# Four edits to a two-layer encoder kernel: sixteen early dot products, a dense expert stage for 224 tokens, a later reload, and a top-k over 112 sums

## The chip, the cores and the metric

The kernel runs on one core of one Trainium2 chip. The core has a matmul engine (TensorE, "PE" in the profile; "PEld" is its loading of weights), a vector engine (VectorE, "DVE"), an activation engine (ScalarE, "ACT"), a general engine (GpSimd, "POOL") and a sync engine (SyncE, "SP") that here does nothing but start DMA transfers. Each engine works through its own queue in order and waits on semaphores for the others. The metric is the device time in microseconds.

## The reference

Two layers; in each a token mixer (a recurrent block in layer 0, a convolution block in layer 1) and then an expert block, with a layer norm behind each. 16 learned tokens are put ahead of the 256 of the input, so layer 0 works on 272 tokens and layer 1's mixer drops the 16. The change touches the expert block alone:

```python
def peer_block(xc, w_query, sub_keys, expert_u, expert_v):
    q = (xc @ w_query).reshape(c, PEER_HEADS, 2, PEER_HALF)
    scores = jnp.einsum('chpk,pnk->chpn', q, sub_keys.astype(q.dtype))
    s1, i1 = lax.top_k(scores[:, :, 0], PEER_TOPK)
    s2, i2 = lax.top_k(scores[:, :, 1], PEER_TOPK)
    cand = (s1[..., :, None] + s2[..., None, :]).reshape(c, PEER_HEADS, PEER_TOPK * PEER_TOPK)
    s, flat = lax.top_k(cand, PEER_TOPK)
    idx1 = jnp.take_along_axis(i1, flat // PEER_TOPK, axis=-1)
    idx2 = jnp.take_along_axis(i2, flat % PEER_TOPK, axis=-1)
    expert = idx1 * PEER_N_KEYS + idx2
    g = jax.nn.softmax(s.astype(jnp.float32), axis=-1).astype(xc.dtype)
    act = jax.nn.gelu(jnp.einsum('chkd,cd->chk', expert_u[expert], xc))
    return jnp.einsum('chk,chkd->cd', g * act, expert_v[expert])
```

There are 8 heads, 128 keys a half, so 16,384 experts; each head of a token picks 16 of them. All is float32, 1024 features wide.

## The kernel before

**Dense and gathered tokens.** Most tokens do not gather their experts. For them the block multiplies by all experts: first by U (128 tiles of 128 experts, each 512 KB), then it weighs the result by a matrix that holds the gates of the chosen experts and zeros elsewhere, then it multiplies by V (128 tiles again). `DENSE_U` and `DENSE_V` give how many tokens of a layer go through U and V in this way. The rest go by groups of 16 tokens (`FEW`), 8 heads x 16 tokens on the 128 partitions, 16 steps for their 16 choices: a dot product (a gather of 128 rows of U by an indirect DMA from POOL, `few_rows`, L1013, and one DVE product with a sum, `few_mult`, L1020) and an addition to the output (a gather of 128 rows of V and one DVE multiply-add, `few_add`, L1049). A group's output is folded into the accumulators by 8 narrow matmuls when it is whole (`few_step`, L1093, called in the V loop). There are three kinds. An **early** group (tokens from 256 in layer 0, from 240 in layer 1) has its first dots in the U stage and the rest in V. A **late** group (from 240 in layer 0) has them all in V. A **drawn** group (from 224 and from 208 in layer 1) goes through the dense U, whose activations are dumped to a table in DRAM (`few_dump`, L710, by POOL); in V its 16 activations are drawn from there by 16 small indirect DMAs (`few_draw`, L1030).

**Stages of a layer's expert block**, in order of the program (`peer`, L545): queries; top-k; U1 (tiles 0 to 63 of U); U2 (tiles 64 to 127, while the gates are built and multiplied in, 8 tokens a chunk, `g_unit`, L676); V (tiles 0 to 123, L753); the last four tiles of V in halves.

**A weight tile** (`load_split`, L138) is loaded by SP, rounded on ACT (`hi`), and the remainder `lo = raw - hi` is taken by DVE or POOL. U takes 24 matmuls a tile (hi by x, hi by the remainder of x, lo by x), and the eight with `lo` stand last. V takes 8 wide ones (hi by the weighted activations and their remainder side by side, twice `DENSE_V` columns) and 8 narrow ones (lo). `raw` has four buffers, `hi` three, `lo` two. In U1 POOL takes the remainders up to tile 40 and DVE from tile 41 (`LO_FROM`), since DVE is at the top-k until then; in U2 and V DVE takes all.

**Top-k** (`topk_steps`, L874) runs on DVE: 16 of 128 keys for 16 halves of heads, then 16 of 256 sums for each head, then the indices by one-hot products. The tokens from 128 on are done first, those from 0 to 127 after them; the last seven steps of the second set go one to a tile from tile 41. `softmax` (L932) makes the gates z from tile 54 on. The gates of groups below token 256 are turned to the groups' layout by way of DRAM: a POOL DMA writes (`few_spread`, L992), and another that waits for its landing reads (`few_fetch`, L996).

**Order.** A scheduler orders each engine's queue by what it thinks is ready; `issue_after(x)` holds instructions of the same engine as x behind x, and does nothing on other engines. So a DMA that POOL starts is not held by an ACT instruction. Steps of the gathered groups in V come from a table that `few_plan` (L1058) makes: rows of (group, dot or sum, step), spread evenly over tiles 2 to 111, the draws between.

## Time and profile before

| what | us |
|---|---|
| median of three runs (1806.37 to 1811.37) | 1810.56 |
| the profiled execution | 1811.96 |
| its span, first to last instruction | 1810.2 |
| U1 of layer 0: first and last activation stored | 178.1 and 350.1 |
| V of layer 0: first wide matmul | 553.0 |
| U1 of layer 1: first and last activation stored | 1095.3 and 1267.6 |
| V of layer 1: first wide matmul | 1466.5 |
| DVE busy | 1503.9 |
| ACT busy | 908.9 |
| POOL busy | 483.8 |

Matmuls overlap one another in the profile, so the busy time of one says little; the count of matmuls in a stretch without waits says how fast they follow each other. "Waited for" names what ended an engine's idle time. Times at a row's start are microseconds from the start of the span.

### The profile page before, as it was taken

What the parts mean: (1) busy time and instruction counts of PE and PEld (TensorE: products, weight loads), DVE (VectorE), ACT (ScalarE), POOL (GpSimd) and SP (SyncE); (2) the same over time, 40 slices, a digit from 0 to 9 for tenths busy, and PEclk for the clock granted to TensorE, in tenths of its full rate; (3) what the DMA queues carried; (4) which work ended last, traced back from release to release, by engine and by line L of the source; (5) the groups of instructions that cost most, each with busy time, mean ns of one, the idle gap of its engine ahead of it and who ended that gap; (6) DMA issues with size and microseconds to landing.
All of it is one profiled execution on the core that took longest, in us unless ns stands there. A gap on an engine that the chain in (4) does not pass through costs nothing.

```text
span 1810.2 us, 34904 instructions
## 1 busy us (share of the span) xinstructions
PE 1760.8 (97%) x13484; PEld 1685.9 (93%) x13484; DVE 1503.9 (83%) x2727; ACT 908.9 (50%) x1492; POOL 483.8 (27%) x328
## 2 busy tenths in 40 slices
PE   8999999999999999999998999999999999999996
PEld 7899999999999999999887899999999999999996
DVE  7786998889997777787699769998889968878875
ACT  5554444554445444885432645445454445544452
POOL 1102993100002332221000017962100035634210
PEclk9999999999999999999999999999999999999998
DMA  5446667755557888887541356578555568989973
GB/s 198 163 152 161 195 195 248 253 164 165 169 171 280 307 306 289 293 305 251 192 133 65 105 175 182 182 240 279 186 173 184 172 247 324 329 310 316 321 259 120
DMA packets 112439, 396.41 MB, mean 219 GB/s; under 512 B 13584, under 2 KB 14992, under 8 KB 112144
## 3 DMA queue, kind: packets, MB, share of 16 engines
q1 hardware_dynamic: 91632, 324.74, 53.7%
q0 software_dynamic: 20640, 69.43, 10.8%
q8 instruction: 106, 1.74, 0.4%
q14 instruction: 61, 0.50, 0.1%
HBM read 387.14 MB, written 6.98 MB: 218 GB/s over the span
## 4 chain that ended last, share of the span: by engine, by line
PE 82%; DVE 9%; DMA 3%; POOL 2%; issue 2%; ACT 1%; POOLq 0%; DVEq 0%; SPq 0%; ACTq 0%
PE u L180 40%; PE acc L732 21%; PE acc L736 12%; PE u L216 3%; DVE cy L1224 2%; POOL lo L152 2%; DVE odd L1224 2%; PE g L682 1%; PE g L683 1%; DVE lo L152 1%; DMA raw<-peer_v 1%; DMA rows<-u_rows,ids 1%; PE sps L578 1%; PE var L856 0%; PE acc L770 0%
## 5 line engine op out<-in xcount | busy, mean ns | idle before, releaser
L145 ACT ACTIVATE hi<-raw 128x1024 fp32r<-128x1024 f32 x556 | 588.6, 1059 | 625.3 <-PE u L180 190.9
L152 DVE TENSOR_TENSOR lo<-raw,hi 128x1024 fp32r<-128x1024 f32 x474 | 579.9, 1226 | 173.6 <-PE acc L736 74.7
L180 PE MATMUL u<-xs,hi 128*128 128x240 f32 (+2 forms) x4544 | 569.1, 277 | 0.6 <-DVE xs L379 0.6
L180 PEld LDWEIGHTS u<-xs,hi 128*128 128x128 f32 x4544 | 537.5, 189 | 1.5 <-DVE xs L379 1.2
L732 PE MATMUL acc<-w,hi 128*128 128x480 f32 (+1 forms) x1984 | 448.0, 368 | 4.8 <-ACT hi L145 2.9
L732 PEld LDWEIGHTS acc<-w,hi 128*128 128x128 f32 x1984 | 355.1, 189 | 29.2 <-ACT hi L145 3.2
L180 PE MATMUL u<-xs,lo 128*128 128x240 f32 (+2 forms) x2272 | 308.2, 277 | 5.4 <-POOL lo L152 3.2
L180 PEld LDWEIGHTS u<-xs,lo 128*128 128x128 f32 x2272 | 280.5, 189 | 7.5 <-POOL lo L152 4.2
L736 PEld LDWEIGHTS acc<-w,lo 128*128 128x128 f32 x2048 | 269.4, 191 | 13.5 <-DVE lo L152 5.8
L736 PE MATMUL acc<-w,lo 128*128 128x240 f32 (+1 forms) x2048 | 272.1, 274 | 4.4 <-DVE lo L152 4.4
L152 POOL TENSOR_TENSOR lo<-raw,hi 128x1024 fp32r<-128x1024 f32 x82 | 209.8, 2580 | 100.6 <-ACT hi L145 73.0
L1015 POOL DMA_INDIRECT rows<-peer_v,ids x80 | 122.3, 1529 | 237.6 <-DVE few_out L1056 171.6
L1015 POOL DMA_INDIRECT rows<-u_rows,ids x48 | 59.9, 1249 | 379.2 <-DVE act_b L702 216.0
L216 PE MATMUL u<-x,raw 128*128 128x272 f32 x480 | 114.7, 399 | 5.3 <-DMA x<-h 5.3
L216 PEld LDWEIGHTS u<-x,raw 128*128 128x128 f32 x480 | 92.9, 194 | 24.8 <-DMA raw<-w_in 5.2
L1056 DVE SCALAR_TENSOR_TENSOR few_out<-rows,act,few_out 128x1024 f32<-128x1024 f32 x75 | 96.0, 1280 | 0.0
L689 ACT ACTIVATE act_b<-g 128x432 f32<-128x432 f32 (+41 forms) x56 | 21.9, 390 | 108.8 <-DVE act_b L652 97.4
L665 DVE TENSOR_TENSOR AB<-iota,iT 128x2048 f16<-128x2048 f16 x56 | 68.1, 1219 | 0.1
L1022 DVE SCALAR_TENSOR_TENSOR rows<-rows,wide 128x1024 f32<-128x1024 f32 x48 | 58.5, 1219 | 4.2 <-DMA rows<-u_rows,ids 4.2
L682 PE MATMUL g<-AB 128*128 128x128 f16 x448 | 56.6, 220 | 0.0
L683 PE MATMUL g<-Bl,AB 128*128 128x128 f16 x448 | 56.0, 219 | 0.0
L713 POOL COPY own<-act_b 128x512 f32<-128x512 f32 (+2 forms) x6 | 5.4, 935 | 182.1 <-ACT act_b L698 182.1
(284 smaller groups left out, 1778.6 us busy)
## 6 DMA issues: line engine op xcount, KB each, us to landing
raw<-peer_u SPq DMA_DIRECT2D x256, 512.0 KB, 4.2
raw<-peer_v SPq DMA_DIRECT2D x248, 512.0 KB, 5.1
raw<-w_query SPq DMA_DIRECT2D x28, 512.0 KB, 4.0
raw<-pw SPq DMA_DIRECT2D x22, 512.0 KB, 3.5
raw<-w_in SPq DMA_DIRECT2D x16, 512.0 KB, 4.1
raw<-w_out SPq DMA_DIRECT2D x8, 512.0 KB, 3.9
raw<-peer_v SPq DMA_DIRECT2D x16, 256.0 KB, 4.5
wide<-wide SPq DMA_DIRECT2D x5, 512.0 KB, 4.3
```

The lines of the kernel that those rows point to most:

```text
L145: self.act_hi = nc.scalar.activation(hi, raw, AF.Copy).ins
L152: i = e.tensor_tensor(lo[:, s], raw[:, s], hi[:, s].bitcast(F32), op=OP.subtract)
L180: self.mm = nc.tensor.matmul(ps[:, :n], l[:, k, :], xs(k, r)[:, :n], start=start, stop=stop)
L216: self.mm = self.nc.tensor.matmul(ps[:, :n], raw[:, k, :], x[:, k, :n], start=k == 0, stop=k == NB - 1)
L665: nc.vector.tensor_tensor(AB.rearrange("p x c (a b) -> p (x c) a b", b=2), keys, iT[:, c0 // HC].rearrange("p x c b -> p (x c) b")[:, :, N ...
L682: nc.tensor.matmul(ps[:, c, :], A, Bh, start=True, stop=False)
L683: nc.tensor.matmul(ps[:, c, :], A, Bl, start=False, stop=True)
L732: self.mm = nc.tensor.matmul(acc[b][:, :2 * n].rearrange("p (a t) -> p a t", a=2), hi, w[:, :, :n], start=j == 0, stop=j == NK - JG - 1, s ...
L736: self.mm = nc.tensor.matmul(main[b][:, :n], hi if p_ else lo, w[:, i, :n], start=False, stop=j == NK - 1 and not p_, skip_group_check=True)
L1015: self.nc.gpsimd.indirect_dma_start(out=t, out_offset=None, in_=table, in_offset=bass.IndirectOffsetOnAxis(ap=few["ids"][:, i, k:k + 1], a ...
L1056: nc.vector.scalar_tensor_tensor(few["out"], t, w, few["out"], op0=OP.mult, op1=OP.add)
L1224: nc.vector.scalar_tensor_tensor(z, h, w, z, op0=OP.mult, op1=OP.add)
```

## The change

In layer 0 V becomes dense for 224 tokens instead of 240, and the group from 224 is drawn, as in layer 1. The early groups do all 16 dots in U1, from tile 41 on, four steps in five tiles; their gelu stands at the end of U1. From tile 42 on every third remainder of U1 is POOL's. The draws of V begin at tile 6, not 2. The reload of the block's input `xr` for the residual is held behind the load of V tile 119. The second search of the top-k goes over the 112 sums in which one of the two ranks is below 4 (a sum with both ranks 4 or more has at least 24 others that are no smaller), and the indices are worked out from the shorter list by four more DVE instructions.

```diff
-DENSE_U, DENSE_V = (240, 240), (240, 208)
-EARLY, LATE, DRAWN = ((256,), (240,)), ((240,), ()), ((), (224, 208))
-DOTS_FROM, DOTS, AHEAD, LO_FROM = 48, 10, 2, 41
+NEAR = 4
+DENSE_U, DENSE_V = (240, 240), (224, 208)
+EARLY, LATE, DRAWN = ((256,), (240,)), ((240,), ()), ((224,), (224, 208))
+DOTS_FROM, AHEAD, LO_FROM = 41, 2, 41
...
-            self.nc.sync.dma_start(raw[:, i * w:(i + 1) * w], part)
+            self.last_load = self.nc.sync.dma_start(raw[:, i * w:(i + 1) * w], part).ins
...
-                    if j == LO_FROM:
+                    if j == DOTS_FROM - 3:
                         for few in early:
                             self.few_load(sp, few, "kept", 1)
...
-                    k, step = divmod(3 * (j - DOTS_FROM), 4)
-                    if early and 0 <= k < DOTS + AHEAD and step < 3:
+                    k, step = divmod(4 * (j - DOTS_FROM), 5)
+                    if early and 0 <= k < TOPK + AHEAD and step < 4:
                         with tc.issue_after(self.dve_lo.ins), tc.issue_after(self.lo_ins.ins):
-                            self.few_dot(sp, early[0], k, DOTS, AHEAD)
+                            self.few_dot(sp, early[0], k, TOPK, AHEAD)
...
+                    if j == JA - 1:
+                        for few in early:
+                            nc.scalar.activation(few["act"], few["act"], AF.Gelu_apprx_tanh)
...
-                self.linears([U[j] for j in range(JA)], xs, nu, lambda j: FULL if j >= LO_FROM else (("p", 1024),), u_store)
+                self.linears([U[j] for j in range(JA)], xs, nu, lambda j: FULL if j >= LO_FROM and j % 3 else (("p", 1024),), u_store)
...
-                        for i in range(2):
-                            nc.sync.dma_start(xr[:, 4 * i:4 * i + 4, :], self.saved[:, 4 * i:4 * i + 4, :])
+                        with tc.issue_after(self.last_load):
+                            for i in range(2):
+                                nc.sync.dma_start(xr[:, 4 * i:4 * i + 4, :], self.saved[:, 4 * i:4 * i + 4, :])
...
-        cand = sp.tile([P, H, K, K], F32, tag="cand", name="cand", bufs=1)
-        nc.vector.tensor_tensor(cand[:m], sv[:m, :, 0, :, None].to_broadcast([m, H, K, K]),
-                                sv[:m, :, 1, None, :].to_broadcast([m, H, K, K]), op=OP.add)
+        cand = sp.tile([P, H, NEAR * K + (K - NEAR) * NEAR], F32, tag="near", name="cand", bufs=1)
+        for part, rows, cols in ((cand[:m, :, :NEAR * K], slice(0, NEAR), slice(0, K)),
+                                 (cand[:m, :, NEAR * K:], slice(NEAR, K), slice(0, NEAR))):
+            shape = [m, H, rows.stop - rows.start, cols.stop]
+            nc.vector.tensor_tensor(part.rearrange("p h (a b) -> p h a b", b=cols.stop),
+                                    sv[:m, :, 0, rows, None].to_broadcast(shape),
+                                    sv[:m, :, 1, None, cols].to_broadcast(shape), op=OP.add)
...
+        nc.vector.tensor_scalar(far, fp, cut, cut, op0=OP.max, op1=OP.subtract)
         nc.vector.tensor_scalar(pu[:m, 0], fp, 4, None, op0=OP.logical_shift_right)
-        nc.vector.tensor_scalar(pu[:m, 1], fp, 15, None, op0=OP.bitwise_and)
+        nc.vector.tensor_scalar(far, far, 2, None, op0=OP.logical_shift_right)
+        nc.vector.tensor_scalar(pu[:m, 1], fp, float(NEAR * K), float(K - NEAR), op0=OP.is_lt, op1=OP.mult)
+        nc.vector.tensor_tensor(pu[:m, 0], pu[:m, 0], far, op=OP.max)
+        nc.vector.scalar_tensor_tensor(pu[:m, 1], pu[:m, 1], NEAR - 1, fp, op0=OP.bitwise_or, op1=OP.bitwise_and)
...
-                for k in range((DOTS if few in early else TOPK if few["drawn"] else 0) if i == 0 else 0, TOPK)]
+                for k in range(0 if i or few in late else TOPK, TOPK)]
...
+            if s == ahead and not late:
+                self.warm(AF.Abs_reciprocal_sqrt)
...
-                        self.few_gelu(few, few is (early + late)[-1])
+                        self.few_gelu(few, few is late[-1])
...
-            lo, hi = begin + 14 * g, at[rows.index((few, 1, 0)) + ahead] - 3
+            lo, hi = 6 + 12 * g, at[rows.index((few, 1, 0)) + ahead] - 3
```

How the instructions stand now is seen at three places. First POOL in U1 of layer 0, from tile 24 of U on before: `rows` are the gathers of the early group, `z` first the write of the turned gates to DRAM and then the read of them.

```order
L152 TENSOR_TENSOR lo<-raw,hi 128x1024 x16
L1015 DMA rows<-u_rows,ids_1619 128x1024 x8
L994 DMA z_240_1627<-z 16x8x16
L998 DMA z_1624<-z_240_1627 128x16
L1015 DMA rows<-u_rows,ids_1619 128x1024 x8
```

The same place after the change, from the remainder of tile 51 on (the remainders below are those of tiles 51, 54, 57 and 60):

```order
L153 TENSOR_TENSOR lo<-raw,hi 128x1024
L1032 DMA rows<-u_rows,ids_1619 128x1024 x2
L153 TENSOR_TENSOR lo<-raw,hi 128x1024
L1032 DMA rows<-u_rows,ids_1619 128x1024 x3
L1011 DMA z_240_1627<-z 16x8x16
L1011 DMA z_224_1634<-z 16x8x16
L1015 DMA z_1624<-z_240_1627 128x16
L1015 DMA z_1630<-z_224_1634 128x16
L153 TENSOR_TENSOR lo<-raw,hi 128x1024
L1032 DMA rows<-u_rows,ids_1619 128x1024 x2
L153 TENSOR_TENSOR lo<-raw,hi 128x1024
```

Before, no remainder stood behind the gates' DMAs on POOL; now that of tile 57 does, with two writes and two reads ahead of it (three and three in layer 1). Second, DVE in U1 of layer 0, before, from the remainder of tile 43 to that of tile 52:

```order
L152 TENSOR_TENSOR lo<-raw,hi 128x1024
L924 TENSOR_TENSOR oh<-oh,s_3436 128x2048
L152 TENSOR_TENSOR lo<-raw,hi 128x1024
L924 TENSOR_TENSOR oh<-oh,s_3436 128x2048
L152 TENSOR_TENSOR lo<-raw,hi 128x1024
L927 TENSOR_REDUCE idx<-oh 128x128
L152 TENSOR_TENSOR lo<-raw,hi 128x1024
L927 TENSOR_REDUCE idx<-oh 128x128
L152 TENSOR_TENSOR lo<-raw,hi 128x1024 x4
L1022 SCALAR_TENSOR_TENSOR rows,act_1620<-rows,wide 128x1024
L152 TENSOR_TENSOR lo<-raw,hi 128x1024
```

And after, from the remainder of tile 44 to that of tile 49 (`rows,act` is a dot product):

```order
L153 TENSOR_TENSOR lo<-raw,hi 128x1024
L939 TENSOR_TENSOR oh<-oh,s_3462 128x2048
L1039 SCALAR_TENSOR_TENSOR rows,act_1620<-rows,wide 128x1024
L939 TENSOR_TENSOR oh<-oh,s_3462 128x2048
L1039 SCALAR_TENSOR_TENSOR rows,act_1620<-rows,wide 128x1024
L153 TENSOR_TENSOR lo<-raw,hi 128x1024
L942 TENSOR_REDUCE idx<-oh 128x128
L1039 SCALAR_TENSOR_TENSOR rows,act_1620<-rows,wide 128x1024
L153 TENSOR_TENSOR lo<-raw,hi 128x1024
L942 TENSOR_REDUCE idx<-oh 128x128
L1039 SCALAR_TENSOR_TENSOR rows,act_1620<-rows,wide 128x1024
L153 TENSOR_TENSOR lo<-raw,hi 128x1024
```

The dots now stand between the last steps of the top-k, where one remainder stood after each step before. Third, SP in layer 1, before, from the load of the early group's tokens (`wide`) in U1:

```order
L1043 DMA wide<-wide_240_12651 128x1024
L135 DMA raw<-peer_u 128x1024 x121
L135 DMA raw<-peer_v 128x1024 x6
L1043 DMA wide<-wide_240_12651 128x1024
L135 DMA raw<-peer_v 128x1024 x56
L759 DMA xr<-saved_11873 128x1024 x2
L135 DMA raw<-peer_v 128x1024 x62
```

and after:

```order
L1060 DMA wide<-wide_240_12747 128x1024
L136 DMA raw<-peer_u 128x1024 x121
L136 DMA raw<-peer_v 128x1024 x120
L764 DMA xr<-saved_11961 128x1024 x2
L136 DMA raw<-peer_v 128x1024 x4
```

The second `wide` of layer 1 is gone, and `xr` has moved from behind V tile 61 to behind V tile 119, where layer 0 had it before and has it now.

More of the change, by code (lines that the diff above doesn't have):

```diff
@@ L894, in topk_steps @@
         for h in range(H):
-            s = cand[:m, h].rearrange("p a b -> p (a b)")
+            s = cand[:m, h]
             v, i = fv[:m, h, :], fi[:m, h, :]
-            r = sp.tile([P, K * K], F32, tag="r2", name="r2", bufs=1)
+            r = sp.tile([P, NEAR * K + (K - NEAR) * NEAR], F32, tag="r2", name="r2", bufs=1)
             nc.vector.max(v[:, 0:8], s)
@@ L907, in topk_steps @@
         fp = fi[:m].rearrange("p h k -> p (h k)")
+        far = sp.tile([P, H * K], U32, tag="far", name="far", bufs=1)[:m]
+        cut = float(NEAR * K - NEAR * NEAR)
+        nc.vector.tensor_scalar(far, fp, cut, cut, op0=OP.max, op1=OP.subtract)
         nc.vector.tensor_scalar(pu[:m, 0], fp, 4, None, op0=OP.logical_shift_right)
-        nc.vector.tensor_scalar(pu[:m, 1], fp, 15, None, op0=OP.bitwise_and)
+        nc.vector.tensor_scalar(far, far, 2, None, op0=OP.logical_shift_right)
+        nc.vector.tensor_scalar(pu[:m, 1], fp, float(NEAR * K), float(K - NEAR), op0=OP.is_lt, op1=OP.mult)
+        nc.vector.tensor_tensor(pu[:m, 0], pu[:m, 0], far, op=OP.max)
+        nc.vector.scalar_tensor_tensor(pu[:m, 1], pu[:m, 1], NEAR - 1, fp, op0=OP.bitwise_or, op1=OP.bitwise_and)
         pf = sp.tile([P, 2 * H * K, 2], F16, tag="pf", name="pf", bufs=1)
@@ L953, in few_new @@
                "z": kp.tile([P, 1, TOPK], F32, name=f"z{t0}")}
+        if few["drawn"]:
+            few["turn"] = kp.tile([P, TOPK], U32, name=f"turn{t0}")
         if t0 < 2 * P:
@@ L1086, in few_plan @@
         for g, few in enumerate(drawn):
-            few["turn"] = vp.tile([P, TOPK], U32, name=f"turn{few['t0']}")
-            lo, hi = begin + 14 * g, at[rows.index((few, 1, 0)) + ahead] - 3
+            lo, hi = 6 + 12 * g, at[rows.index((few, 1, 0)) + ahead] - 3
             self.steps += [(lo + k * (hi - lo) // TOPK, lambda few=few, k=k: self.few_draw(few, k)) for k in range(TOPK)]
```

## The prediction

> **What bounds the kernel now.** I read the page's busy times first.
>
> ```profile
> PE 1760.8 (97%) x13484; PEld 1685.9 (93%) x13484; DVE 1503.9 (83%) x2727; ACT 908.9 (50%) x1492; POOL 483.8 (27%) x328
> ```
>
> PE is the bound nearly everywhere: it is busy for 97% of the span. So only two things count: how much PE has to do, and how long it waits. Work taken from DVE, such as the shorter top-k, is worth only what PE waited for it. Next I cut V into stretches and counted matmuls. Columns: stretch, length, busy us (count) of PE, PEld, DVE, ACT and POOL, granted clock, DMA share, GB/s.
>
> ```profile
> 595.00:685.00 90.00, 90.00 (x548) 81.82 (x548) 70.32 (x62) 44.59 (x44) 30.26 (x17) 1.00 0.84 304
> 1527.00:1590.00 63.00, 63.00 (x421) 62.71 (x420) 53.42 (x62) 33.73 (x34) 38.76 (x28) 1.00 0.91 331
> 1474.00:1490.00 16.00, 13.94 (x89) 13.36 (x89) 11.05 (x15) 5.29 (x6) 9.44 (x8) 1.00 0.94 348
> 1508.00:1518.00 10.00, 8.61 (x55) 8.23 (x55) 6.56 (x10) 6.11 (x7) 5.17 (x5) 1.00 0.74 270
> 1621.00:1632.00 11.00, 7.88 (x35) 7.10 (x34) 6.83 (x6) 5.43 (x6) 2.10 (x2) 0.69 0.69 257
> 1760.00:1776.00 16.00, 16.00 (x110) 15.94 (x109) 9.56 (x9) 9.00 (x9) 0.00 (x0) 1.00 0.62 200
> ```
>
> The first two are undisturbed V, of layer 0 (480 wide columns) and of layer 1 (416). The next three are layer 1's disturbances. The last is layer 1 when the gathers are over.
>
> **V of layer 0, narrower.** 90.00/548 x 16 = 2.628 us a tile at 480 columns, and 63.00/421 x 16 = 2.394 at 416. The new 448 is half-way, 2.511, so 0.117 less for each of 124 tiles: **-14.5 us**.
>
> ```profile
> L732 PE MATMUL acc<-w,hi 128*128 128x480 f32 x992 | 236.8, 381 | 1.0 <-DVE w L264 1.0
> L732 PE MATMUL acc<-w,hi 128*128 128x416 f32 x992 | 211.1, 355 | 3.8 <-ACT hi L145 2.9 <-DVE w L264 0.9
> L736 PE MATMUL acc<-w,lo 128*128 128x240 f32 x1024 | 136.4, 275 | 0.8 <-DVE lo L152 0.8
> L736 PE MATMUL acc<-w,lo 128*128 128x208 f32 x1024 | 135.7, 274 | 3.7 <-DVE lo L152 3.7
> L770 PE MATMUL acc<-same,few_out 128*128 128x16 f32 x80 | 9.3, 258 | 0.0
> ```
>
> Half the difference of the two wide rows is 12.8 us, the nearer end. The narrow rows are alike at 240 and 208 columns, so nothing comes from them or from the last four tiles, which have only that form. Whether V keeps that pace: layer 0 will gather 64 times in some 110 tiles, (512 KB x (1 + 64/110))/2.511 us = 330 GB/s, as the undisturbed stretch of layer 1 moves (331) without a wait. I add nothing; at 348 GB/s the stretch from 1474 did wait, so up to +5.
> The additional group costs one more fold: 9.3/80 x 16 matmuls = **+1.9**.
>
> **U2 of layer 0** has 28 chunks of gates instead of 30. A chunk stands between two tiles (first matmul of a chunk, and of the tile behind it):
>
> ```profile
> 400.57 0.23 PE L682 MATMUL g<-AB 128*128 128x128 f16 x1
> ...
> 401.45 2.04 PE L180 MATMUL u<-xs,hi 128*128 128x240 f32 x16
> ```
>
> Its matmuls take 401.45 - 400.57 = 0.88; two fewer give **-1.8**.
>
> **V of layer 1: three waits.** By 0.1496 us a matmul, the stretches lost 16.00 - 89 x 0.1496 = 2.7, then 10.00 - 55 x 0.1496 = 1.8, then 11.00 - 35 x 0.1496 = 5.8. Who was waited for, from the waits of 1470:1490, of 1506:1518 and of 1618:1632, with SP's own issue from the timeline:
>
> ```profile
> ACT hi L145 <- DMA raw<-peer_v: 7.9, 2, 6.7
> 1473.34 0.33 SPq L1043 DMA_DIRECT2D wide<-wide  x1
> DVE w L264 <- ACT w L261: 3.4, 1, 3.4
> ACT hi L145 <- DMA raw<-peer_v: 8.7, 4, 7.6
> 1610.82 0.80 SPq L759 DMA_DIRECT2D xr<-saved  x2
> ```
>
> In the first, V tiles came late behind `wide` and the first draws; layer 1 loses that load and draws from tile 6. In the second, ACT was at the early group's gelu; it moves to the end of U1. In the third, the 1 MB of `xr` joined a stage that already moves 331 GB/s; it moves to where 200 GB/s are moved (last stretch). All three should go: **-10.2**. If the new places brought the waits back it would be 0; layer 0 has `xr` at that place now without one.
>
> **U1, both layers.** Here a wait is added. POOL's queue and PE, first layer 0, then layer 1:
>
> ```profile
> 329.38 0.60 POOL L994 DMA_DIRECT2D z<-z  x1 [1.52 <-DVE z L947]
> 333.14 0.58 POOL L998 DMA_DIRECT2D z<-z  x1 [3.17 <-DMA z<-z]
> 331.10 1.06 PE L180 MATMUL u<-xs,lo 128*128 128x240 f32 x8
> 1253.48 0.54 POOL L998 DMA_DIRECT2D z<-z  x1 [1.45 <-DMA z<-z]
> 1249.77 1.06 PE L180 MATMUL u<-xs,lo 128*128 128x240 f32 x8
> L152 POOL TENSOR_TENSOR lo<-raw,hi x82: 2359/2402/4406, 160.0 to 1199.7; 128x1024 fp32r<-128x1024 f32 x82
> ```
>
> The gates are written by POOL, and the read stands until the write has landed. Now the remainder of tile 57 is queued behind this pair, and behind that the gathers and the remainder of tile 60. PE cannot go on: the eight `lo` matmuls of tile 57 began at 331.10 and 1249.77. With two pairs in layer 0 the reads end a trigger later, 333.14 + 0.58 + 0.6 = 334.3; 0.3 to start and 2.4 for the remainder give 337.0, so PE stands 5.9. In layer 1 the third read ends at 1254.02 already; plus 2.7 is 1256.7, PE stands 6.9. Together **+12.8**. This holds if DVE has the gates as early as now; I do not think so.
>
> ```profile
> 285.00:350.00 65.00, 64.27 (x571) 63.78 (x570) 56.24 (x82) 33.01 (x56) 9.84 (x11) 1.00 0.80 271
> L1022 DVE SCALAR_TENSOR_TENSOR rows<-rows,wide 128x1024 f32<-128x1024 f32 x48 | 58.5, 1219 | 4.2 <-DMA rows<-u_rows,ids 4.2
> 292.11 1.22 DVE L924 TENSOR_TENSOR oh<-oh,s 128x2048 f16<-128x2048 f16 x1
> 297.49 2.28 DVE L927 TENSOR_REDUCE idx<-oh 128x128 f32<-128x2048 f16 x1
> 296.35 1.23 DVE L152 TENSOR_TENSOR lo<-raw,hi 128x1024 fp32r<-128x1024 f32 x1 [0.33 <-ACT act_a L608]
> 1160.36 16.21 POOL L152 TENSOR_TENSOR lo<-raw,hi 128x1024 fp32r<-128x1024 f32 x6
> L890 DVE TENSOR_TENSOR cand<-sv x5: 2377/3319/16228, 183.4 to 1158.1; 128x2048 f32<-128x2048 f32 x4, 128x256 f32<-128x256 f32 x1
> rows<-u_rows,ids POOLq DMA_INDIRECT x48, 7.2
> ```
>
> A sum that takes 2.38 at least took 16.23, the one at 1158.1, while POOL ran six remainders: such DVE work stands while POOL's runs. From the remainder of tile 44 to that of 47 DVE now has two products (2 x 1.22), three dots (3 x 1.22), two remainders (2 x 1.23) and a reduction (2.28), 10.8, and 2.4 more while POOL takes tile 45: 13.2 for three tiles of 24 x 65.00/571 = 2.7, less one tile that the second `lo` buffer gives: 2.4 late. Then the tenth dot before the gates waits for rows gathered behind POOL's tile 54, which land 7.2 after issue: some 1.8 more. So 4.2 a layer, **+8.4**; none at the low end, rival C at the high one.
> The granted clock was 0.69 over 11 us around layer 1's waits of 2.2 and less, worth 3.4 at full loss; the new waits are longer. I take 2.2 for each, **+4.4**, between 0 and 6.8: part falls into the wait itself.
> [...]
> Against it stand PE's old waits behind this place (for `lo` of DVE and for the second gates), which a longer wait ahead of them gives DVE time to remove: 1.6 + 0.6 in layer 0, 0.9 in layer 1, **-3.0**:
>
> ```profile
> PEld u L180 <- DVE lo L152: 1.6, 1, 1.6
> PEld tps L1105 <- DVE z L947: 1.2, 2, 0.6
> PEld u L180 <- DVE lo L152: 0.9, 1, 0.9
> PEld u L180 <- POOL lo L152: 1.6, 1, 1.6
> PEld u L180 <- POOL lo L152: 2.6, 4, 1.6
> ```
>
> U1 sums to +22.6.
>
> **Top-k among 112.**
>
> ```profile
> L898 DVE MAX8 fv<-cand x33: 396/410/429, 188.1 to 1183.9; 128x8 f32<-128x256 f32 x33
> ```
>
> Five searches a head, 8 heads, shorter by at most 144/256 of 0.41 us each: up to 9 us of DVE for a set of tokens. All of it ends ahead of tile 41, where POOL takes the remainders and PE does not wait for DVE; I take 0. The four instructions more, and `cand` in two pieces, meet POOL's remainders as above. PE's waits for POOL in U1 (last two rows above, 1.6 + 2.6) could go, -4, or grow by as much.
>
> **The sum:** -14.5 + 1.9 - 1.8 - 10.2 + 22.6 = -2.0. From the profiled 1811.96 that is 1810.0; that execution lies 1.4 over the median of 1810.56, so 1808.6 would stand to the median. I state 1810.
>
> **The rivals.**
> A, forecast: V's gain is given back in U1, at tile 57. Own range 1803 to 1817. Chance 0.42.
> B, faster: the gates are no later than now and the clock holds. Then U1 costs 12.8 - 3.0 = 9.8, the sum is -14.8, 1797; were the queue on POOL less of a bar than its order says, -24.6 and 1787. For it speaks that DVE sheds eight remainders a layer (8 x 1.23) for six dots more (6 x 1.22); against it, the row of 16.23. Chance 0.30.
> C, slower: DVE and POOL shut each other out in all of U1 from tile 41. DVE's 56.24 become 56.24 - 9.8 + 7.3 = 53.7, and 8 x 2.40 of POOL come on top: 72.9 in 65.0, so 7.9 a layer more, on top of the 4.2 that the dots' late rows and the crowded tiles 44 to 47 cost: +15.8 on the sum, 1824; half of that gives 1816. It decides from the point at which the two together exceed the 65 us. Against it: reductions and small steps may run beside POOL, and DVE catches up while PE waits for tile 57. Chance 0.28, with V of layer 0 slowed by its gathers.
> [...]
> That `xr` or the gelu do not bring what they cost is in A and C: each is worth 6 at most.
>
> **How the numbers follow.** A change under 0.3% (5.4 us) is about what a measurement of this kernel cannot tell from none. A lies nearly whole within it, B below, C above: faster 0.30, same 0.42, slower 0.28. The range runs from B's 1797 to C's full price, 1824.
>
> **What would show it.** Right: in V of layer 0 some 0.157 us a matmul at clock 1.00; in layer 1 no clock under 1.00 near V tile 62 and no `hi` waiting 7 us for `raw`; in each U1 one wait of PE for POOL's `lo` of 5 us or more, with a `z<-z` read just ahead of it on POOL. Wrong: PE waits for POOL in U1 stay under 2 us (B), or PE waits for `lo` at many tiles from 45 on (C), or V of layer 0 shows DMA shares above 0.94 with waits for `raw`.

## The result, and the profile after

The changed kernel takes **1823.80 us** (median of four runs, 1823.02 to 1826.98), the kernel before beside it 1808.78: a ratio of 1.0086 (1.0065 to 1.0107). It is slower, where no change was forecast (1810.0). The profiled execution took 1824.29, 12.3 more than that of before.

The stages show where. All times are from the timelines: U1 from its first stored activation to its last, U2 from there to V's first wide matmul, V of layer 0 to the first activation of layer 1, V of layer 1 to the end of the span. Each kernel's stages are those of its one profiled execution, which can lie some us from the median (u1_before 4.7 above it, u1_later_turn 4.7 and u1_gates_late 3.1 below), so a difference of 2 us between stages decides nothing by itself.

| | U1, layer 0 | U2 | V | U1, layer 1 | U2 | V to the end |
|---|---|---|---|---|---|---|
| before | 171.9 | 202.9 | 542.3 | 172.3 | 199.0 | 343.7 |
| after | 194.0 | 201.8 | 530.9 | 189.2 | 198.0 | 330.6 |
| difference | +22.1 | -1.1 | -11.4 | +16.9 | -1.0 | -13.1 |
| forecast | +10.2 | -1.8 | -12.6 | +12.4 | 0 | -10.2 |

(The forecast's halves of U1 are its terms by layer: 5.9 and 6.9, twice 4.2, twice 2.2, less old waits of some 2.1 and 0.9.) V and U2 came out nearly as they were worked out; U1 lost 39.0 and not 22.6. V first, in stretches without a fold: length, busy us (count) of PE, PEld, DVE, ACT and POOL, granted clock, DMA share, GB/s.

```profile
595.00:655.00 60.00, 60.00 (x385) 57.42 (x384) 51.69 (x51) 30.83 (x31) 28.23 (x20) 1.00 0.93 336
1500.00:1590.00 90.00, 90.00 (x602) 89.61 (x600) 73.64 (x88) 47.91 (x49) 53.20 (x42) 1.00 0.92 323
1620.00:1650.00 30.00, 30.00 (x203) 29.87 (x202) 24.53 (x25) 14.67 (x15) 14.27 (x10) 1.00 0.88 311
```

60.00/385 x 16 = 2.494 us a tile in layer 0 (2.511 was worked out), at 336 GB/s (330). In layer 1 30.00/203 is a matmul each 0.148 us past tile 62, where the reload of `xr` had been: its waits are gone, and so is the low clock.

Now U1 from tile 41 on: the same row of after and of before in layer 0, then of layer 1.

```profile
285.00:375.00 90.00, 74.62 (x577) 73.58 (x576) 76.42 (x106) 33.58 (x58) 47.97 (x31) 0.87 0.67 234
1212.00:1297.00 85.00, 73.44 (x609) 72.52 (x608) 69.34 (x88) 35.13 (x60) 51.22 (x32) 0.94 0.72 249
```

```profile
285.00:353.00 68.00, 65.90 (x583) 65.22 (x582) 59.21 (x85) 33.93 (x58) 9.84 (x11) 1.00 0.76 259
1205.00:1271.00 66.00, 65.32 (x582) 64.97 (x581) 58.53 (x74) 33.56 (x57) 15.01 (x18) 1.00 0.76 266
```

583 matmuls took 68 us and 577 now take 90. POOL went from 9.84 to 47.97 us (remainders, gathers), the clock from 1.00 to 0.87. What PE's weight loads waited for after the change, first from 280 to 376, then from 1205 to 1297 (sum, times, longest):

```profile
PEld u L181 <- DVE lo L153: 5.9, 2, 3.2
PEld u L181 <- POOL lo L153: 5.8, 2, 3.8
PEld tps L1123 <- DVE z L962: 4.8, 1, 4.8
...
PEld u L181 <- POOL lo L153: 5.3, 1, 5.3
PEld u L181 <- DVE lo L153: 4.8, 2, 3.2
PEld tps L1123 <- DVE z L962: 1.8, 1, 1.8
```

28.4 us of waits, against 3.7 in the rows of before (1.6, 1.2 and 0.9). Most of the rest of the 39.0 is half clock: in the trace 76 matmuls of layer 0's U1 and 45 of layer 1's follow their predecessor at about 0.21 us, where 0.112 is the pace, which is 7.8 and 4.5 us; before there were 3 and 3. Some 2.5 us are in neither.

The place that the forecast named, as it went in layer 0, on POOL, DVE and PE:

```profile
326.83 2.88 POOL L153 TENSOR_TENSOR lo<-raw,hi 128x1024 fp32r<-128x1024 f32 x1 [0.84 <-PE u L181]
329.85 1.77 POOL L1032 DMA_INDIRECT rows<-u_rows,ids  x1
331.92 1.03 POOL L1032 DMA_INDIRECT rows<-u_rows,ids  x1 [0.30 <-issue]
...
342.48 1.16 POOL L1011 DMA_DIRECT2D z<-z  x2 [7.20 <-DVE z L962]
346.05 1.14 POOL L1015 DMA_DIRECT2D z<-z  x2 [2.41 <-DMA z<-z]
347.21 2.35 POOL L153 TENSOR_TENSOR lo<-raw,hi 128x1024 fp32r<-128x1024 f32 x1
```

```profile
334.85 0.23 DVE L954 TENSOR_SCALAR d<-z 128x128 f32<-128x128 f32 x1 [0.37 <-ACT z L952]
338.53 1.23 DVE L1039 SCALAR_TENSOR_TENSOR rows<-rows,wide 128x1024 f32<-128x1024 f32 x1 [3.45 <-DMA rows<-u_rows,ids]
...
339.68 0.95 DVE L955 RECIPROCAL d<-d 128x128 f32<-128x128 f32 x1
...
341.89 0.29 DVE L962 TENSOR_TENSOR z<-z,sm 128x128 f32<-128x128 f32 x1
342.24 0.42 PE L1123 MATMUL tps<-ident,z 96*128 96x96 f32 x1 [4.62 <-DVE z L962]
```

Read from the top: a gather stands behind POOL's remainder of tile 54 and starts at 329.85; its row lands near 338.5; a dot that waits for it stands on DVE between two steps of the gates (3.45); so the gates are whole at 342.2, PE has waited 4.8 for them, and only then do POOL's write, read and remainder of tile 57 follow, for which PE waits another 3.8.

### The profile page after: what moved, and what is told of

The parts are those of the page before. It is cut to its first block, busy times and chain, and to the rows that moved or that the text cites. A ratio compares the mean times of both kernels' runs of the same rounds, so it can differ in the third digit from the quotient of the medians.

```text
span 1822.5 us, 35020 instructions
## 1 busy us (share of the span) xinstructions
PE 1754.8 (96%) x13468; PEld 1696.3 (93%) x13468; DVE 1520.8 (83%) x2762; ACT 905.5 (50%) x1493; POOL 592.0 (32%) x390
## 4 chain that ended last, share of the span: by engine, by line
PE 72%; DVE 17%; DMA 3%; issue 2%; POOL 2%; ACT 2%; SPq 0%; POOLq 0%; DVEq 0%; ACTq 0%
PE u L181 33%; PE acc L736 20%; PE acc L740 12%; PE u L217 3%; DVE cy L1242 2%; POOL lo L153 2%; DVE odd L1242 2%; DVE oh L939 2%; DMA raw<-peer_v 2%; PE g L686 1%; PE g L687 1%; DMA rows<-u_rows,ids 1%; DVE lo L153 1%; DVE rows L1039 1%; ACT hi L146 1%
## 5 line engine op out<-in xcount | busy, mean ns | idle before, releaser
L153 DVE TENSOR_TENSOR lo<-raw,hi 128x1024 fp32r<-128x1024 f32 x458 | 559.0, 1224 | 145.0 <-PE u L181 53.4
L181 PE MATMUL u<-xs,hi 128*128 128x240 f32 (+2 forms) x4544 | 579.4, 280 | 1.0 <-DVE xs L380 0.6
L736 PE MATMUL acc<-w,hi 128*128 128x448 f32 (+1 forms) x1984 | 430.8, 359 | 1.9 <-DVE w L265 1.9
L153 POOL TENSOR_TENSOR lo<-raw,hi 128x1024 fp32r<-128x1024 f32 x98 | 247.4, 2538 | 132.6 <-ACT hi L146 83.4
L740 PE MATMUL acc<-w,lo 128*128 128x224 f32 (+1 forms) x2048 | 269.8, 273 | 3.4 <-DVE lo L153 3.4
L1032 POOL DMA_INDIRECT rows<-peer_v,ids x96 | 145.4, 1515 | 225.0 <-DVE few_out L1073 144.0
L1073 DVE SCALAR_TENSOR_TENSOR few_out<-rows,act,few_out 128x1024 f32<-128x1024 f32 x90 | 115.1, 1279 | 0.0
L1032 POOL DMA_INDIRECT rows<-u_rows,ids x48 | 73.7, 1536 | 51.6 <-DVE rows L1039 41.6
L693 ACT ACTIVATE act_b<-g 128x488 f32<-128x488 f32 (+39 forms) x54 | 21.0, 388 | 104.7 <-DVE act_b L656 100.1
L1049 POOL DMA_INDIRECT act<-own,turn x48 | 60.8, 1267 | 29.0 <-DVE turn L1048 13.9
```

The source lines that it names most:

```text
L153: i = e.tensor_tensor(lo[:, s], raw[:, s], hi[:, s].bitcast(F32), op=OP.subtract)
L181: self.mm = nc.tensor.matmul(ps[:, :n], l[:, k, :], xs(k, r)[:, :n], start=start, stop=stop)
L736: self.mm = nc.tensor.matmul(acc[b][:, :2 * n].rearrange("p (a t) -> p a t", a=2), hi, w[:, :, :n], start=j == 0, stop=j == NK - JG - 1, s ...
L740: self.mm = nc.tensor.matmul(main[b][:, :n], hi if p_ else lo, w[:, i, :n], start=False, stop=j == NK - 1 and not p_, skip_group_check=True)
L1032: self.nc.gpsimd.indirect_dma_start(out=t, out_offset=None, in_=table, in_offset=bass.IndirectOffsetOnAxis(ap=few["ids"][:, i, k:k + 1], a ...
L1049: self.nc.gpsimd.indirect_dma_start(out=few["act"][:, k:k + 1], out_offset=None, in_=few["table"].rearrange("p j (t o) -> (p j t) o", o=1) ...
```

## The experiments

Each kernel has the edits shown or named, longer ones cut at "..."; if nothing else is said, it starts from the changed kernel ("after"). The figures are the median, the ratio to the kernel before with its interval, and stages as in the table above.

### The two edits of U1, undone one by one

```diff
-self.linears([U[j] for j in range(JA)], xs, nu, lambda j: FULL if j >= LO_FROM and j % 3 else (("p", 1024),), u_store)
+self.linears([U[j] for j in range(JA)], xs, nu, lambda j: FULL if j >= LO_FROM else (("p", 1024),), u_store)
```

> The changed kernel, but every remainder of U1 from tile 41 on is DVE's again (no third one on POOL); the sixteen early dots stay. Theory P (the loss in U1, 38.9 us over both layers against before, comes from POOL's eight remainders a layer: tile 57 queued behind the gates' DMAs, gathers queued behind remainders, DVE stopped while POOL runs): U1 of both layers back to within 6 us of before, time 1786 to 1797. Theory D (it comes from the six more and earlier dots on DVE's queue): DVE gets 8 x 1.22 = 9.8 more a layer, time 1820 to 1840.

```diff
-DOTS_FROM, AHEAD, LO_FROM = 41, 2, 41
+DOTS_FROM, DOTS, AHEAD, LO_FROM = 48, 10, 2, 41
...
-                    k, step = divmod(4 * (j - DOTS_FROM), 5)
+                    k, step = divmod(3 * (j - DOTS_FROM), 4)
...
-                for k in range(0 if i or few in late else TOPK, TOPK)]
+                for k in range((DOTS if few in early else TOPK if few["drawn"] else 0) if i == 0 else 0, TOPK)]
...
```

> The changed kernel, but with ten early dots from tile 48 on in U1, the other six and the gelu in V, as before; every third remainder stays POOL's. P: PE still stands 5 us or more for POOL's remainder of tile 57 in each U1, U1 15 to 25 us over before, time 1800 to 1812. D: U1 within 6 of before, time 1786 to 1794.

Both edits together undone:

> The changed kernel with both of U1's edits undone (remainders all DVE's from tile 41, ten early dots from tile 48, the other six and the gelu in V); V of layer 0 at 224, the later reload, the later draws and the top-k among 112 stay. P and D: U1 as before, V and U2 as measured in the changed kernel (-11.4, -1.1, -0.9, -10.6, and -2.4 at the end), less up to 4.5 for the two small waits in V of layer 1 that come back: 1782 to 1788. If V's gain hung on the early dots: 1795 or more.

| | median | ratio | U1, layer 0 | U1, layer 1 | V of layer 1 to the end |
|---|---|---|---|---|---|
| after | 1823.80 | 1.0086 (1.0065 to 1.0107) | 194.0 | 189.2 | 330.6 |
| u1_lo_dve | 1793.16 | 0.9901 (0.9878 to 0.9924) | 177.3 | 175.5 | 330.3 |
| u1_ten_dots | 1820.85 | 1.0057 (1.0037 to 1.0078) | 187.3 | 181.9 | 337.4 |
| u1_before | 1792.25 | 0.9895 (0.9878 to 0.9912) | 171.8 | 172.1 | 337.4 |

It is POOL's share. Sixteen dots alone cost U1 8.6 over both layers (177.3 + 175.5 - 344.2), POOL's remainders alone 25.0, both together 39.0, which is 5.4 more than the two. Theory D falls: with eight remainders more a layer on DVE the kernel is 30 us faster. Theory P had the share too small: u1_ten_dots was expected at 1800 to 1812 and came 9 above. u1_before was expected at 1782 to 1788 and missed by 4, of which the dots left in V are some 2.5 (7 against the 4.5 allowed); the rest is not explained. The waits of PE in V of layer 1 there (1460 to 1760), and DVE:

```profile
PEld acc L737 <- DVE lo L153: 4.8, 1, 4.8
1474.99 1.23 DVE L1036 SCALAR_TENSOR_TENSOR rows<-rows,wide 128x1024 f32<-128x1024 f32 x1 [6.05 <-DMA rows<-u_rows,ids]
```

V opens with six dots of the early group, whose first row lands late, and the remainder behind it waits. So the sixteen dots in U1 earn 7 us in V of layer 1, about what they cost in U1.

### The gates' DMAs moved behind the remainders

```diff
-                    if j == JA - 6 - len(picked):
-                        with tc.issue_after(last.ins):
+                    if j == JA - 3:
+                        with tc.issue_after(self.lo_ins.ins):
                             self.few_spread(near, "z", picked[0][3][:, None])
...
-                    if j == JA - 2:
-                        with tc.issue_after(last.ins):
+                    if j == JA - 1:
+                        with tc.issue_after(self.lo_ins.ins):
                             self.few_fetch(near, "z")
```

> The changed kernel, but POOL writes the turned gates behind the remainder of tile 60 and reads them behind that of tile 63, so that the remainder of tile 57 has no DMA of the gates ahead of it. If the queue on POOL is what costs at tile 57: PE's waits for POOL there (3.8 and 5.3, and 2.0 at tile 61 of layer 0) go, with part of the half clock behind them, time 1808 to 1815. If the gates themselves are late on DVE and PE waits for them anyway: time 1819 to 1826, with the wait of PE before the transposed gates (4.8 and 1.8) as long as it was.

1811.88, 1.0013 (0.9999 to 1.0027); U1 187.3 and 184.6, 11.3 less than after. The waits of PE from 280 to 376:

```profile
PEld u L181 <- DVE lo L153: 5.9, 2, 3.2
PEld tps L1123 <- DVE z L962: 3.9, 1, 3.9
PEld u L181 <- POOL lo L153: 2.8, 1, 2.8
```

The wait at tile 57 is gone, as the forecast's order on POOL said it would be, and one of 2.8 for that of tile 63 takes part of its place. The gates are nearly as late as they were (3.9); in layer 1 no wait for POOL's remainders is left, and the one for the gates is 3.4, where it was 1.8.

### What of POOL's share is the queue, the shared access, and PE's own wait

u1_none leaves the remainders of eight tiles a layer out. The next two put work back on POOL at the same places, between the same gathers, for which nobody waits; so that it is not dropped, its result overwrites one column of the early group's gates.

```diff
+                def extra():
+                    with tc.issue_after(self.gather or self.lo_ins.ins), tc.issue_after(self.lo_ins.ins):
+                        self.lo_ins = nc.gpsimd.tensor_tensor(spare, spare, early[0]["x"][:, :960], op=OP.add)
```

and in u1_pool_set, in place of the addition:

```diff
+                        for _ in range(2):
+                            nc.gpsimd.memset(spare[:, :959], 1.0)
+                            self.lo_ins = nc.gpsimd.tensor_tensor(spare[:, 959:960], spare[:, 959:960], spare[:, 0:1], op=OP.add)
```

> The changed kernel, but the remainders of U1's tiles 42, 45, 48 ... 63 are left out altogether: their eight matmuls take the remainder of the tile before (no DVE and no POOL work for them). It is the base of the next two runs: DVE has as much to do as in the changed kernel, POOL has only gathers and the gates' DMAs. All theories: U1 within 4 us of before in each layer (171.9 and 172.3 there, 194.0 and 189.2 in the changed kernel), time 1785 to 1792.

> As u1_none, and where POOL had a remainder it now adds two SBUF tiles of 960 columns for which nobody waits. S (DVE's work with two inputs in SBUF and POOL's shut each other out): U1 10 us or more over u1_none in layer 0, 6 or more in layer 1, with waits of PE for lo of DVE near tiles 42 to 48. Q (gathers queued behind POOL's work land late): 3 to 8 over u1_none in each, the same as in u1_pool_set. R (only PE's own waits for POOL's remainders cost): within 2 of u1_none.

> As u1_none, and where POOL had a remainder it now fills 959 columns twice with a constant (no input) and adds one column to one. S: within 2 us of u1_none. Q: as u1_pool_pair, if the fills take as long. R: within 2 of u1_none.

| | median | ratio | U1, layer 0 | U1, layer 1 | both, over before |
|---|---|---|---|---|---|
| u1_none | 1788.99 | 0.9881 (0.9856 to 0.9905) | 174.9 | 174.8 | +5.5 |
| u1_pool_set | 1795.52 | 0.9917 (0.9894 to 0.9940) | 179.4 | 178.0 | +13.2 |
| u1_pool_pair | 1804.29 | 0.9979 (0.9955 to 1.0004) | 184.5 | 180.9 | +21.2 |
| after | 1823.80 | 1.0086 (1.0065 to 1.0107) | 194.0 | 189.2 | +39.0 |

POOL's work from 284 to 372 in u1_pool_pair, then in u1_pool_set (count, busy us, mean ns):

```profile
L604 POOL TENSOR_TENSOR spare<-spare,wide 128x960 f32<-128x960 f32 x8 | 18.4, 2296 | 0.2
```

```profile
L605 POOL MEMSET spare<- 128x959 f32 x16 | 14.7, 919 | 0.5
L606 POOL TENSOR_TENSOR spare<-spare 128x1 f32<-128x1 f32 x16 | 6.3, 392 | 1.3
```

18.4 and 21.0 us: POOL is kept about as long by either. The dots on DVE in the same stretch, first pair, then set:

```profile
L1053 DVE SCALAR_TENSOR_TENSOR rows<-rows,wide 128x1024 f32<-128x1024 f32 x16 | 22.9, 1439 | 2.8 <-DMA rows<-u_rows,ids 2.8
```

```profile
L1055 DVE SCALAR_TENSOR_TENSOR rows<-rows,wide 128x1024 f32<-128x1024 f32 x16 | 19.5, 1221 | 6.5 <-DMA rows<-u_rows,ids 6.5
```

None of the three theories has it alone. Beside fills a dot takes 1221 ns (1219 in u1_none), beside additions 1439. Step by step, half clock included: **5.5** for the sixteen dots with eight remainders fewer a layer, **7.7** for a POOL that is busy, **8.0** for additions in place of fills, and **17.8** for PE's own need of POOL's remainder; u1_gates_late, which takes the gates' DMAs out of the way of one such remainder a layer, got 11.3 back. The medians give 6.5, 8.8 and 19.5 for the last three steps. Another order of the steps could share the sum out otherwise. The second step is the least clear: DVE's waits for rows grow only from 5.9 (u1_none) to 6.5, and the one-column additions have two SBUF inputs, too, so that Q is not shown to be all of it. The third step is the one that goes with the 1439 ns beside additions and the 1221 beside fills, and in this order of steps it is worth 8.0 of the 39.0.

### PE takes the gates a tile later

```diff
-                    if 0 < t <= len(picked) and not odd:
+                    if 0 < t <= len(picked) and odd:
                         with tc.issue_after(last.ins), tc.issue_after(self.mm.ins):
                             self.topk_out(*picked[t - 1], iT, ghT, glT)
```

> As u1_lo_dve (sixteen dots, all remainders of U1 from tile 41 on DVE), and PE turns the gates one tile of U later, after tiles 57 and 59, not 56 and 58. If the gates are late on DVE by less than a tile: the waits of PE for z (3.0 in layer 0, 1.9 and 0.3 in layer 1 of u1_lo_dve) go, U1 174 and 173, time 1786 to 1790. If the remainders behind are what is late: the wait moves to them, time as u1_lo_dve, 1791 to 1795.

1796.42, 0.9918 (0.9901 to 0.9935); U1 176.6 and 174.7, but U2 of layer 0 203.3 (201.8). The row of PE's waits from 280 to 376 is now one:

```profile
PEld u L181 <- DVE lo L153: 7.8, 8, 2.3
```

The 3.0 us for z went into eight waits for remainders (5.3 in five before): DVE is the one that is late, and what PE asks for first shows it. No gain; the median lies 1.4 above the higher of the two ranges expected.

### Layer by layer, the width of V, the reload

In dots_by_layer the dots are chosen by layer, ten from 48 in layer 0 and sixteen from 41 in layer 1; v_240 sets DENSE_V back to (240, 208) and draws no group in layer 0; xr_alone adds to the kernel before the one line that holds the reload behind the last load.

> As u1_lo_dve in layer 1, and in layer 0 the early dots of before (ten from tile 48, the other six in V). If the stages add up: layer 0 as u1_before (171.8, 203.0, 531.8), layer 1 as u1_lo_dve (175.5, 198.1, 302.4), 2.7 under u1_lo_dve, time 1788 to 1792. If they do not: 1793 or more.

> As u1_lo_dve, but V of layer 0 is dense for 240 tokens again, and the group from 224 is not drawn. By the forecast's terms the matmuls of V cost 14.5 more, one fold and its waits less (1.9 and the 2 to 3 us of PE waiting for lo that V of layer 0 shows now), two chunks of gates more (1.8): from the first matmul of V of layer 0 to the first activation of layer 1 541 to 543 (530.2 in u1_lo_dve), time 1804 to 1808. If gathers are what V of layer 0 pays for and the width is not: under 1800.

> The kernel before, with the later reload of x as its one change. If the reload was the cause of the third wait in V of layer 1: PE's waits of 2.2 and 1.4 near V tile 62 and the half clock there go, V of layer 1 306 to 307.5 (312.5 before), time 1802 to 1805. If the loads are late there for another reason: 1808 to 1811, with a wait at the same place.

dots_by_layer: **1791.21**, 0.9897 (0.9876 to 0.9919), layer 0 171.2, 201.5, 533.7 and layer 1 176.2, 198.0, 330.5. It is 17 us under the kernel before and the lowest median of those that leave nothing out, though u1_before, u1_lo_dve and pinned_112 (below) lie within 2 us of it, which these runs do not separate. v_240: 1805.79, 0.9986 (0.9974 to 0.9998), V 543.5 against 530.2 in u1_lo_dve: the narrower V is worth 13.3. xr_alone: 1805.22, 0.9976 (0.9963 to 0.9989), 0.2 over its range, V of layer 1 338.6, 5.1 less than before. The stretch with tile 62, in the kernel before and in xr_alone:

```profile
1605.00:1640.00 35.00, 31.89 (x194) 31.00 (x193) 24.52 (x24) 15.14 (x16) 14.49 (x10) 0.90 0.83 300
```

```profile
1605.00:1640.00 35.00, 35.00 (x235) 34.86 (x234) 27.54 (x28) 16.75 (x18) 15.71 (x12) 1.00 0.92 323
```

### The shorter search

top_256 is u1_lo_dve with all 256 sums searched; top_112_alone is the kernel before with the search among 112.

> As u1_lo_dve (sixteen dots, all remainders of U1 from tile 41 on DVE), but the second search of the top-k goes over all 256 sums again. K0 (the shorter search is worth nothing, as DVE's top-k ends ahead of tile 41 anyway): U1 within 2 us of u1_lo_dve (177.3 and 175.5), time 1791 to 1796. K1 (DVE comes late to tile 41 without it, so that the shorter search pays for the early dots): U1 4 us or more longer in layer 0, the more so as both sets of tokens search there, time 1797 to 1808.

> The kernel before, with the search among 112 sums as its one change. If the shorter search is worth only what PE waited for it in that kernel: DVE ready for tile 41 some 11 us earlier in layer 0 (its last search ends at 282 in before), U1 within 1 us of before (171.9 and 172.3), time 1806 to 1811. If PE's waits for POOL in U1 come from DVE's top-k: U1 168 to 171, time 1801 to 1806.

top_112_alone: 1809.35, 0.9997 (0.9986 to 1.0009), U1 172.5 and 171.6: nothing, as forecast. top_256: 1800.96, 0.9951 (0.9934 to 0.9968), and U1 of layer 0 186.9, 9.6 more than u1_lo_dve, by one wait at tile 41:

```profile
PEld u L181 <- DVE lo L153: 10.5, 1, 10.5
```

Why in this kernel and not in that one? A product of DVE in layer 0's top-k, of 128x512, in the kernel before, in after and in top_256:

```profile
232.26 5.11 DVE L924 TENSOR_TENSOR oh<-oh,s 128x512 f16<-128x512 f16 x1
```

```profile
231.78 18.88 DVE L939 TENSOR_TENSOR oh<-oh,s 128x512 f16<-128x512 f16 x1
```

```profile
230.94 21.29 DVE L929 TENSOR_TENSOR oh<-oh,s 128x512 f16<-128x512 f16 x1
```

and what POOL does meanwhile, in before and in after:

```profile
231.43 0.86 POOL L994 DMA_DIRECT2D pos<-idx  x1
232.32 7.31 POOL L152 TENSOR_TENSOR lo<-raw,hi 128x1024 fp32r<-128x1024 f32 x3
239.57 0.62 POOL L998 DMA_DIRECT2D pos<-pos  x1
```

```profile
231.23 1.47 POOL L1011 DMA_DIRECT2D pos<-idx  x2
232.72 7.10 POOL L153 TENSOR_TENSOR lo<-raw,hi 128x1024 fp32r<-128x1024 f32 x3
239.76 1.14 POOL L1015 DMA_DIRECT2D pos<-pos  x2
240.92 12.01 POOL L153 TENSOR_TENSOR lo<-raw,hi 128x1024 fp32r<-128x1024 f32 x5
```

The group newly drawn in layer 0 has its positions turned by way of DRAM, too: a second pair of DMAs among POOL's remainders. POOL falls behind and runs five in a row, from 240.92 to 252.93, and the product ends only at 250.66. That is 13.8 us more; the shorter search gives some 10 of them back (layer 0's last search ends at 282.0 in before and at 271.9 in top_112_alone). To test it, the later groups' positions go behind tile 40:

```diff
-                            self.few_spread(near, "pos", picked[0][2])
+                            self.few_spread(near[:1], "pos", picked[0][2])
+                    if j == LO_FROM + 1:
+                        with tc.issue_after(self.lo_ins.ins):
+                            self.few_spread(near[1:], "pos", picked[0][2])
...
-                            self.few_fetch(near, "pos")
-                        for few in near:
+                            self.few_fetch(near[:1], "pos")
+                        for few in near[:1]:
                             self.few_ids(few, few["pos"])
+                    if j == LO_FROM + 12:
+                        with tc.issue_after(self.lo_ins.ins):
+                            self.few_fetch(near[1:], "pos")
+                        for few in near[1:]:
+                            self.few_ids(few, few["pos"])
```

> As top_256, but the positions of the groups behind the first (in layer 0 of the group drawn from 224) are written and read by POOL behind tile 40, not beside those of the first group at tiles 21 to 24, where POOL has a remainder for every tile. If that second pair of DMAs makes POOL run its remainders without a gap, so that DVE's product stands 21 us at 231 and DVE comes late to tile 41: the product stands under 8, PE's wait of 10.5 at tile 41 of layer 0 goes, U1 175 to 179 there (186.9 in top_256), time 1789 to 1796. If the search over 256 is late by itself: U1 of layer 0 185 or more, time 1799 to 1803.

> As u1_lo_dve, with the positions written and read apart as in apart_256. If DVE's late start at tile 41 of layer 0 is what is left of the cost of sixteen dots: U1 of layer 0 174 to 175 (177.3 in u1_lo_dve; 174.4 in v_240, where no second pair stands), time 1788 to 1791.5. If not: 177, time 1792 to 1795.

Both missed: 1811.62, 1.0007 (0.9993 to 1.0020), and 1809.86, 1.0003 (0.9989 to 1.0017). The product stood only 5.1 and 5.4 us, but DVE's work on the later groups' numbers was ordered ahead of tile 41's remainder, and waits for the read. What DVE waited for in apart_112, from 270 to 300:

```profile
DVE ids L1029 <- DMA pos<-pos: 16.9, 1, 16.9
```

An experiment that took one wait away and made another. With that work held behind the remainder of tile 53:

```diff
-                        for few in near[1:]:
-                            self.few_ids(few, few["pos"])
+                        with tc.issue_after(self.dve_lo.ins):
+                            for few in near[1:]:
+                                self.few_ids(few, few["pos"])
```

> As apart_256, and DVE works out the numbers of the later groups behind the remainder of tile 53; in apart_256 that work stood ahead of tile 41's remainder and waited for the read from DRAM. If the 256 sums are late only through the long stand (18.9 and 21.3 us in kernels with two pairs of DMAs at tiles 21 to 24, 5.1 to 5.4 with one): no wait of over 1 us at tile 41, U1 of layer 0 174 to 178, time 1790 to 1796. If they are late by themselves: 3 us or more at tile 41, U1 180 or more, time 1797 or more.

> As apart_112, with that work behind the remainder of tile 53. If DVE's late start at tile 41 is what is left of the cost of sixteen dots in layer 0: U1 there 174 to 175, 175.5 or less in layer 1, time 1788 to 1791.5. If not: 177 and 175.5, time 1792 to 1795.

pinned_256: 1793.42, 0.9912 (0.9885 to 0.9938), U1 of layer 0 175.0 (186.9 in top_256) and no wait at tile 41. pinned_112: 1793.07, 0.9898 (0.9874 to 0.9921), 174.5 there, but 179.3 in layer 1 (175.5 in u1_lo_dve), so no gain over u1_lo_dve. In that layer PE waits 2.0 for a remainder behind a DMA that POOL issued late (at 1172.23, after 2.8 us in which it waited for nothing that the profile shows), and the clock halves twice; why the DMA is late stays open. The product in pinned_256:

```profile
232.50 5.41 DVE L938 TENSOR_TENSOR oh<-oh,s 128x512 f16<-128x512 f16 x1
```

Without the second pair 256 and 112 sums take the same time. The search is worth 9.6 us of U1 only where the drawn group's DMAs have made DVE late.

## Why the prediction was wrong

In short: the gain of V and U2 was right (24.6 forecast, 26.6 measured), and U1's loss of 22.6 should have been 39.0. The places of U1's waits were mostly right. What failed is the size of two terms: the clock's (+4.4, measured 11.8) and that of the waits (18.2 net of the old ones, measured 24.7). 1823.8 lies just within the stated range, at its end.

- **V of layer 0, narrower (-14.5, fold +1.9).** Right: -11.4 by the stages, -13.3 by v_240. Some of the "up to +5" came: PE waits 4.0 us for DVE's `lo` there, at a DMA share of 0.93.
- **U2 (-1.8).** -1.1.
- **V of layer 1 (-10.2).** -13.1 to the end. The reload's 5.8 is 5.1 in xr_alone; the early group's dots and gelu, put at 4.5, are 7 by u1_ten_dots against after, and 3 us come from the very end (last section). These make 15, so they overlap by some 2; that was not taken apart.
- **U1, tile 57 (+12.8).** Right in kind: the gates' DMAs do stand ahead of the remainder, and PE waits 3.8 and 5.3 for it. It is less than 12.8 because PE stands for the late gates first (4.8 and 1.8); the two together are 15.7, and 12.8 with the 1.8 a layer for the late row would be 16.4. The wait for tile 63's remainder in layer 0, 2.0, was not in the sum: there ACT's rounding stands behind the early group's gelu, which waits 3.4 for the last dot (to 365.79), and POOL's remainder behind that. (u1_ten_dots, without this gelu, waits 2.4 at the same tile, where the tile of U landed late.) Moving the DMAs gave back 11.3 with its share of the clock.
- **U1, DVE late (+8.4) and old waits gone (-3.0).** Mis-sized. For tiles 44 to 47 the text had 2.4 a layer; PE waits 3.2 in each, at tile 47. Two waits are missing from it: 1.6 for DVE's `lo` just behind U1's last tile in layer 1, one of the old waits that were to go, and 2.7 at tile 41 in layer 0. There DVE takes a small step, which works out row numbers of the gathers, ahead of tile 41's remainder:

```profile
285.49 2.35 DVE L1021 TENSOR_SCALAR ids<-pos,slot 128x16 uint32<-128x16 f32 x1
```

The same step takes 0.23 in u1_lo_dve; here POOL takes the remainder of tile 42 beside it (285.39 to 287.81). DVE comes to it without a lead, since the product of 18.9 us has used that up (in top_112_alone DVE is idle for 8.1 us ahead of tile 41's remainder). But u1_lo_dve has the long product, too, and PE waits only 0.3 there, so it takes POOL's share as well. The text looked for what POOL's new remainders do at tiles 44 to 47, and not at the first of them nor at what the drawn group puts on POOL at tile 21.

- **U1, the clock (+4.4).** This is the step that failed most: 11.8 (7.8 + 4.5 less 0.5). The text charged 2.2 for each of two waits, those at tile 57, and nothing for the waits that it had itself at tiles 44 to 47 and for the gates. In after the half clock follows seven waits, the shortest of 2.0; that behind the last of layer 0 falls in U2. The price was about right for one wait: a step of 3.41 us at half clock (last section) costs 1.7, half of it, by estimate, if PE is busy in all of it (18 matmuls in the one from 290.40 in after, 33 at full clock in the one from 335.59 in u1_lo_dve). But in layer 0 the wait for the gates and that for tile 57, one behind the other, cost four such steps in a row:

```profile
338.19:341.60 3.41, 0.00 (x0) 0.00 (x0) 3.00 (x8) 1.62 (x3) 0.00 (x0) 1.00 0.81 333
341.60:355.25 13.65, 9.52 (x43) 9.24 (x44) 10.47 (x19) 2.33 (x6) 6.69 (x7) 0.50 0.37 127
```

- **Top-k (0).** Right alone, wrong in this kernel (9.6 in layer 0).
- **Rival C** named the mechanism of POOL and DVE shutting each other out, and gave 1816 to 1824. Its time was right in part by luck. It put 7.9 to 15.8 on the sum for that mechanism, where the pair of experiments has 8.0 between fills and additions; the clock and the waits at tiles 41 and 63 are the rest. Its sign, waits for `lo` at many tiles from 45 on, did not come: PE waits for `lo` four times in layer 0 and three times in layer 1. What spoke against it holds in part: in after a reduction at 304.14 takes 2.27 with a remainder of POOL beside its last 0.6 us (2.28 at 297.49 in before, with none), but the small step above took 2.35 for 0.23. And its times start from 1808.6, those of the forecast and of B from 1811.96; from there C would be 1818 to 1826. **Rival B** gave 1787 to 1797 with POOL's remainders in place. u1_lo_dve lies there (1793), but without those remainders, so it says nothing for B.

## What to carry to other kernels

Work moved to an idle engine joins that engine's queue: list what starts from it (here gathers that DVE waits for, 3.45 us in the row at 338.53, and DMAs that wait for a landing, 2.41 at 346.05), and count each wait that follows, with its half clock (11.8 us in both U1 here), not the first alone. An edit in one stage can take the slack that another edit lives on: ask of each added DMA which instructions it comes between, even 20 tiles ahead of the place in question. Undoing one part of a bundle is the cheapest test: one line, given back, made a loss of 0.9% a gain of 1.0%.
